# Block sums of two MLP phases on VectorE, RWKV output weights loaded during the scan, two affine maps on ScalarE

## The chip, the core and the metric

The kernel runs on one core of a Trainium2 chip. Its engines work through one instruction queue each, in order: TensorE (PE, with its weight loads listed apart as PEld), VectorE (DVE), ScalarE (ACT), GpSimd (POOL) and SyncE (SP, which issues most DMAs). The metric is the device time of the core in microseconds, as the median of several runs; less is better. The profile is one execution of its own.

## What is computed

The program is a decoder trunk of two layers for 1024 positions of width 1024, all in float32. Layer 0 mixes tokens with an RG-LRU, layer 1 with RWKV-7; each layer then attends to a memory of 256 tokens and ends with an MLP of width 4096:

```python
# every layer: x += post_norm(mixer(pre_norm(x)))
#              x += post_norm(mem_xattn(pre_norm(x), norm(mem)))
#              x += post_norm(sqrelu_mlp(pre_norm(x)))
def sqrelu_mlp(h, w_up, w_down):
    return jnp.square(jax.nn.relu(h @ w_up)) @ w_down

def rwkv7_mixer(x, mu, w_rkv, w0, w1, w2, a0, a1, a2, g1, g2, k_k, k_a, ..., w_o):
    ...
    a = jax.nn.sigmoid(a0 + (xa @ a1) @ a2)
    ...
    k = k * (1.0 + (a - 1.0) * k_a)
    ...
    _, ys = lax.scan(step, state0, seq_inputs)      # one state of 64x64 per head
    ...
    return (out * g) @ w_o
```

## The kernel before

**Float32 by halves.** A product of float32 matrices is made of three matmuls of a reduced format. For that an operand of 128x1024 is split (`split`, L230 to L234): ACT casts it into a high half (L232), and DVE subtracts that from the original for the low half (L233); with `eng` given, another engine does the subtraction. `mm3` (L317 to L319) issues the three matmuls. "A split" is below the DVE or POOL part, "a cast" the ACT part.

**The MLP with seven products.** Both halves of the MLP multiply 2x2 blocks with seven block products instead of eight (p1 to p7). Four of the seven take a sum of blocks as an operand: t1 to t4. In the up half (`cphase`) the sums of the activations are made in `combine_in` (L375 to L422): t1 and t2 on DVE, t3 (L416) and t4 (L420) on POOL, two instructions of 128x1024 each, and `parts` splits each operand once its sum is there. The place where this stands between the phases is called the up seam; L482 and L487 are ACT copies of finished up products there.

In the down half (`mlp`, from L925) there are 4 groups of 7 products; each product is 48 matmuls of 512 columns, in four passes p of 12, one for each of four accumulators. The weights' blocks are loaded by SP (`weights`), the activations' blocks come back from memory (`block`). For the sums t1 to t4 of the weights' blocks `sums` issues two POOL instructions of 128x1024 (L1002), in place, one product ahead of their splits; `parts` splits the two A blocks and the two B blocks of the next product, all on DVE but the second B block of a summed operand, which goes to POOL. After each pass the accumulator is copied (ACT, L1059) or added (DVE, L1061) into `acc`: an evacuation. The sums of activations that are spilled for later groups (`out`, L957 to L962) are made on POOL and stored from POOL's DMA queue; the last of them lie at the start of the down phase.

**What sets the order.** A scheduler orders the instructions, each engine's apart. The lines within `with self.line("down")` are kept in the order of the program on each engine; so the evacuations, the splits and the sums of the down phase stand as they are written.

**RWKV.** `decay` makes the tile a, with the map a = 0.5 a + 0.5 (L1268), and `prep_rest` the factor kp = k_a a + (1 - k_a) (L1289), both on DVE for all 8 tiles f. `evac_r` (L1452) takes the r product out of the accumulator. The v phase makes the v product for f = 0 to 7; then a scan of 16 chunks follows. SP loads a chunk pair's tiles ahead of it (L1559 to L1591, and the z tiles of L1563); in the chunk, DVE (L1739, L1747) and PE (L1715, L1720, L1745, L1753) pass a state on. After the scan `tphase` multiplies with the output weights `b_w_o`. Weights come through a plan of tiles: `take` hands out a tile and `fetch` (L266) loads `depth + ahead` tiles further (SP, L252) and splits `depth` of them. During the v phase three tiles of `b_w_o` are loaded and two of them split; the other five are loaded at the scan's end. All these tiles, the raw ones too, come from one pool of "u" buffers of 128x1024.

Of the kernel before, what the change touches and what calls it, by code (L numbers as in the profile page):

```python
# [9 lines left out]
AF = mybir.ActivationFunctionType  # L10
# [39 lines left out]
class Net:  # L50
# [321 lines left out]
    def combine_in(self, xs, hf, g, B):  # L372
# [40 lines left out]
            nc.vector.tensor_sub(t2[i], b22[i], t1[i])  # L413
        parts("t2", t2)
        for i in range(2):
            nc.gpsimd.tensor_tensor(t3[i], t2[i], b11[i], ALU.subtract)  # L416
        parts("t3", t3)
        parts("b22", b22)
        for i in range(2):
            nc.gpsimd.tensor_tensor(t4[i], b21[i], t2[i], ALU.subtract)  # L420
        parts("t4", t4)
        del B["raw"]  # L422

# [512 lines left out]
    def mlp(self, layer, xt, raw, post, late=None):  # L936
# [58 lines left out]

        def sums(m):

            if m < len(seq) and seq[m][3] in DSUMS:
                f = rows[seq[m][0]]
                o, x, y = DSUMS[seq[m][3]]  # L1000
                for i in range(2):
                    nc.gpsimd.tensor_tensor(f[o][i], f[x][i], f[y][i], ALU.subtract)  # L1002

        def parts(m):

            if m >= len(seq):
                return [lambda: None] * 4
            ab = ops[m] = [], []
            name = seq[m][3]
            fs = rows[seq[m][0]][DSUMS[name][0] if name in DSUMS else {"b11": (0, 0), "b21": (1, 0), "b22": (1, 1)}[name]]  # L1010
            a = [lambda t=t: ab[0].append(self.split(t)) for t in blocks.pop(m)]
            return a + [lambda t=t, e=e: ab[1].append(self.split(t, eng=e))
                        for t, e in zip(fs, (None, nc.gpsimd if name in DSUMS else None))]

        def loads():
            block(0)
# [13 lines left out]
        for m, (g, name, qa, qb, bank, begins, ends, to) in enumerate(seq):  # L1030
# [6 lines left out]
            for i in soon(m, 23):  # L1037
                block(i + 1)
            A, B = ops.pop(m)
            work = [parts(i) for i in soon(m, 24)]  # L1040
            line = lambda: self.line("down")
            for p in range(4):
                with line():
                    for w in work:
                        for i in ((0, 1), (2,), (3,), ())[p]:
                            w[i]()
                if begins:
                    ps[bank, p] = self.bank(p + 1)
                o = ps[bank, p]
                for j in range(4):  # L1050
                    at = slice((j % 2) * 512 + p * 128, (j % 2) * 512 + p * 128 + 128)
                    bt = slice((j % 2) * 512, (j % 2) * 512 + 512)
                    self.mm3(o, [t[:, at] for t in A[j // 2]], [t[:, bt] for t in B[j // 2]],
                             begins and j == 0, ends and j == 3, skip_group_check=True)
                with line():
                    for e, s, new in to:
                        to_ = acc[e][:, p, s]
                        if new and g == 0:
                            nc.scalar.copy(to_, o)  # L1059
                        else:  # L1060
                            nc.vector.tensor_add(to_, to_, o)  # L1061
                if g == 3 and name == "p3":
                    post(p, acc[0][:, p, :])
                if g == 3 and name == "p7" and layer == 1 and p == 3:

                    sq = [self.small(1) for _ in range(2)]
                    nc.scalar.activation(self.unit()[:, right], acc[1][:, 3, right], AF.Square, accum_out=sq[0])
                if g == 3 and name == "p4":
                    if layer == 1 and p == 3:
                        nc.scalar.activation(self.unit()[:, left], acc[1][:, 3, left], AF.Square, accum_out=sq[1])  # L1070
                        nc.gpsimd.tensor_tensor(sq[0], sq[0], sq[1], ALU.add)
                        post(7, acc[1][:, 3, :], sq[0])
                    else:
                        post(4 + p, acc[1][:, p, :])
            with line():
                for i in soon(m, 23):
                    sums(i + 1)
            if m == 1:
                rest()
            if late and m >= LATE:  # L1080
# [120 lines left out]
def rwkv(self, X, xt, lw_wa, lw_g, post):  # L1201
# [55 lines left out]
    def decay(f):  # L1257
# [7 lines left out]
                self.mm3(p, (wa2[0][r, cs], wa2[1][r, cs]), (hwa[0][r, s], hwa[1][r, s]), True, True)  # L1265
                nc.scalar.activation(t[:, s], p, AF.Tanh, bias=c1(b), scale=0.5)
        nc.vector.tensor_scalar(lw, lw, -LC, -LC, ALU.mult, ALU.add)
        nc.vector.tensor_scalar(a, a, 0.5, 0.5, ALU.mult, ALU.add)  # L1268
        IP = self.unit()
        nc.vector.tensor_tensor_scan(IP, d01, lw, 0.0, ALU.mult, ALU.add)  # L1270
        P = lw
# [14 lines left out]
    def prep_rest(f):  # L1286
        a, P, IP, at = dk.pop(f)
        kp = self.unit()
        nc.vector.tensor_scalar(kp, a, self.col("k_a", f), self.kam[:, f:f + 1], ALU.mult, ALU.add)  # L1289
        sq = self.unit()  # L1290
        nc.scalar.activation(sq, at, AF.Square)
        nc.vector.scalar_tensor_tensor(a, a, self.col("k_k", f), IP, ALU.mult, ALU.mult)
# [385 lines left out]
    for i, fs in enumerate(turns):  # L1678
        for f in turns[i + 1] if i < 6 else []:
            early(f)  # L1680
        self.fphase(I["b_w_rkv"][0, 2], fs, xv, evac_v, spread=i == 0)
        aside(len(TURNS) + 6 + i)
        if fs[-1] == LD:
# [5 lines left out]
        scan_scale(c)  # L1689
        scan_gram(c, range(4))  # L1690
    load_late(0)
    self.depth, self.ahead = 2, 3
    self.psum_layout("banks")
    for h in range(2):
        nc.gpsimd.memset(cst[0]["sv"][hr[h], :, h, :], 0.0)
    for c in range(16):
        if c % 2 == 0:
            with (ExitStack() if c else self.behind()):
                load(c // 2 + 1)
                load_solved(c // 2 + 1)  # L1700
                load_late(c // 2 + 1)
        s = cst[c]
        sv, gts, mv, pcc, xtc, pcs = s["sv"], s["gts"], s["mv"], s["pcc"], s["xt"], s["pcs"]
        dbv = self.db[:, 0:128].rearrange("p (q a t) -> p q a t", a=2, t=8)[:, :, c % 2, c // 2:c // 2 + 1]
# [52 lines left out]
        post_mean(c)  # L1757
    post_var(15)
    post_norm(15)
    self.psum_layout("mixed")  # L1760

    self.later += [lambda: flip_out(14), lambda: flip_out(15)]
    w = I["b_w_o"][0]
    rows = []
# [53 lines left out]
```

## Time and profile before

| | |
|---|---|
| time, median of 3 runs | 2984.14 us (2982.08 to 2985.70) |
| the profiled execution | 2987.84 us, span 2986.1 us |
| TensorE's mean granted clock | 0.983 of 2.4 GHz |
| busy, share of the span | PE 96%, PEld 80%, DVE 62%, ACT 45%, POOL 39% |
| down phase of layer 0 | about 1010 to 1360 us |
| up seams | about 710 to 735 and 2355 to 2385 us |
| v phase, scan | about 1640 to 1800, 1800 to 2000 us |
| down phase of layer 1 | about 2660 to 2986 us |

The profile counts microseconds from the start of the span. "Busy" is the time in which an engine executed; a row of the order of time merges like instructions in sequence, and a wait stands in brackets with the instruction that ended it. PEclk is the clock granted to TensorE, 1.00 being 2.4 GHz and 0.50 being 1.2 GHz; a stretch in which both occur has a mean between them. Since PE is busy in all but 4% of the span, the waits of PE are what is to be looked at, each with what ended it.

### The profile page before, as it was taken

To read this page: it belongs to the slowest core of one execution; us is meant where nothing else is said; L and a number is where in the kernel's file an instruction comes from. 1 tells how busy PE (TensorE), PEld (TensorE's weight loads), DVE (VectorE), ACT (ScalarE), POOL (GpSimd) and SP (SyncE) were. 2 spreads that over 40 slices of the span, in tenths; PEclk is the share of its full clock that TensorE was granted. 3 is DMA by queue.
4 is the path that set the end of the run, shared out by engine and by line. 5 is a ranking of instruction groups with operands and counts; after the bars stand their busy time and mean duration, and the time that the engine had idled before them with its cause. 6 is when DMAs were issued, how large, how long until landed. Compare 5 with 4: busy or idle time off the path is not lost. (4 is left out here: it accounts for less than half of the span.)

```text
span 2986.1 us, 42754 instructions
## 1 busy us (share of the span) xinstructions
PE 2860.0 (96%) x16987; PEld 2381.4 (80%) x16987; DVE 1842.6 (62%) x2020; ACT 1349.5 (45%) x1967; POOL 1151.9 (39%) x1055
## 2 busy tenths in 40 slices
PE   7999999999999999999999998999999999999998
PEld 6888798887888878787778677878788788887886
DVE  5576552556455578887685627883355745557878
ACT  6464342545444543347452534442244544454333
POOL 2000110024766554351486215652002466655445
PEclk9999999999999999999999999999999999999999
DMA  7212362123444554432656989852312244455443
GB/s 256 75 50 83 101 196 71 60 74 104 161 150 143 192 196 148 159 116 92 175 162 187 235 228 227 182 136 92 99 52 83 89 155 150 152 203 183 155 169 113
DMA packets 383847, 421.91 MB, mean 141 GB/s; under 512 B 91440, under 2 KB 294432, under 8 KB 383648
## 3 DMA queue, kind: packets, MB, share of 16 engines
q1 hardware_dynamic: 371616, 379.19, 42.3%
q0 software_dynamic: 11568, 39.41, 3.6%
q8 instruction: 133, 2.18, 0.3%
q14 instruction: 66, 0.54, 0.1%
q10 hardware_dynamic: 464, 0.59, 0.1%
HBM read 283.79 MB, written 134.74 MB: 140 GB/s over the span
## 5 line engine op out<-in xcount | busy, mean ns | idle before, releaser
L233 DVE TENSOR_TENSOR u<-u,u 128x1024 fp32r<-128x1024 f32 (+1 forms) x518 | 845.9, 1657 | 360.6 <-ACT u L232 342.3
L232 ACT CAST u<-u 128x1024 fp32r<-128x1024 f32 (+1 forms) x550 | 542.7, 1022 | 405.7 <-POOL u L1002 107.8
L318 PE MATMUL q<-u,u 128*128 128x512 f32 (+2 forms) x1824 | 700.4, 385 | 17.3 <-DVE u L233 17.2
L317 PE MATMUL q<-u,u 128*128 128x512 f32 (+2 forms) x1824 | 694.5, 387 | 13.6 <-ACT u L232 7.5
L319 PE MATMUL q<-u,u 128*128 128x512 f32 (+2 forms) x1824 | 693.6, 384 | 0.5 <-DVE u L233 0.5
L317 PE MATMUL p<-u,u 128*128 128x512 f32 (+1 forms) x1728 | 659.4, 384 | 21.3 <-ACT u L232 9.8
L318 PE MATMUL p<-u,u 128*128 128x512 f32 (+1 forms) x1728 | 657.6, 381 | 6.4 <-DVE u L233 6.4
L319 PE MATMUL p<-u,u 128*128 128x512 f32 (+1 forms) x1728 | 656.0, 380 | 3.7 <-DVE u L233 3.7
L318 PEld LDWEIGHTS q<-u,u 128*128 128x128 f32 (+1 forms) x1824 | 345.9, 190 | 88.6 <-DVE u L233 23.0
L317 PEld LDWEIGHTS q<-u,u 128*128 128x128 f32 (+1 forms) x1824 | 344.7, 189 | 85.9 <-ACT u L232 9.2
L328 POOL TENSOR_SCALAR s<-s 128x1 f32<-128x1 f32 x98 | 40.3, 411 | 941.3 <-ACT u L326 921.8
L317 PEld LDWEIGHTS p<-u,u 128*128 128x128 f32 x1728 | 331.3, 192 | 86.3 <-ACT u L232 13.8
L319 PEld LDWEIGHTS q<-u,u 128*128 128x128 f32 (+1 forms) x1824 | 345.3, 189 | 67.6 <-DVE u L233 0.7
L318 PEld LDWEIGHTS p<-u,u 128*128 128x128 f32 x1728 | 332.1, 192 | 67.9 <-DVE u L233 10.5
L319 PEld LDWEIGHTS p<-u,u 128*128 128x128 f32 x1728 | 331.5, 192 | 65.6 <-DVE u L233 5.2
L1002 POOL TENSOR_TENSOR u<-u,u 128x1024 f32<-128x1024 f32 x64 | 185.3, 2912 | 191.3 <-DVE u L233 165.4
L1061 DVE TENSOR_TENSOR z<-z,q 128x512 f32<-128x512 f32 x192 | 128.1, 679 | 92.3 <-PE q L319 92.3
L430 POOL TENSOR_TENSOR u<-u,u 128x512 f32<-128x512 f32 x96 | 150.9, 1575 | 8.3 <-PE q L318 5.1
L233 POOL TENSOR_TENSOR u<-u,u 128x1024 fp32r<-128x1024 f32 x32 | 80.7, 2523 | 95.3 <-ACT u L232 73.8
L957 POOL TENSOR_TENSOR u<-u,u 128x512 f32<-128x512 f32 x32 | 44.1, 1377 | 154.7 <-ACT u L946 140.5
L319 PE MATMUL q<-z,u 128*128 128x512 f32 x256 | 99.8, 390 | 1.2 <-DVE u L233 1.2
L318 PE MATMUL q<-z,u 128*128 128x512 f32 x256 | 99.6, 389 | 0.0
(258 smaller groups left out, 3458.8 us busy)
## 6 DMA issues: line engine op xcount, KB each, us to landing
u<-d SPq DMA_DIRECT2D x198, 512.0 KB, 4.7
d<-u SPq DMA_DIRECT2D x109, 512.0 KB, 3.3
d<-u POOLq DMA_DIRECT2D x68, 512.0 KB, 3.6
d<-u SPq DMA_DIRECT2D x132, 256.0 KB, 3.4
u<-in_m_w_up SPq DMA_DIRECT2D x64, 512.0 KB, 5.3
u<-in_m_w_down SPq DMA_DIRECT2D x64, 512.0 KB, 7.8
u<-in_c_w_kv SPq DMA_DIRECT2D x32, 512.0 KB, 6.8
u<-d SPq DMA_DIRECT2D x56, 256.0 KB, 6.8
```

The lines of the kernel that those rows point to most:

```text
L232: self.nc.scalar.copy(hv, src)
L233: (eng or self.nc.vector).tensor_tensor(lv, src, hv, ALU.subtract)
L317: mm(o, ah, bh, start=first, stop=False, **kw)
L318: mm(o, ah, bl, start=False, stop=False, **kw)
L319: mm(o, al, bh, start=False, stop=last, **kw)
L328: nc.gpsimd.tensor_scalar(v, ss, 1.0 / n, eps, ALU.mult, ALU.add)
L430: sub = lambda o, x, y: nc.gpsimd.tensor_tensor(o, x, y, ALU.subtract)
L957: tt(s1, r21, r22, ALU.add)
L1002: nc.gpsimd.tensor_tensor(f[o][i], f[x][i], f[y][i], ALU.subtract)
L1061: nc.vector.tensor_add(to_, to_, o)
```

## The change

- In `combine_in`, t3 and t4 are made on DVE.
- In the down phase the sums t1 to t4 are made on DVE, 32 instructions a layer, and the second B blocks are split on DVE as well, 16 a layer. `parts` and `sums` now give lists of work, which is handed out over the four passes: three pieces ahead of pass 0, one ahead of each later pass, what is left after the last. Each piece stands alone in the kept order, so sums and splits stand between the evacuations.
- `decay` makes the map of a on ACT for f above 1, and `prep_rest` makes kp on ACT: 6 and 8 instructions.
- From the v phase's f of 5 on, `depth` and `ahead` are set so that no output weight is fetched there. In the scan, at chunks 5, 7, 9, 11, 13 and 15, they are raised step by step, so that one tile of 128x1024 is loaded at each of the first, and one split at each of the last two; after the scan they have their old values.

```diff
@@ combine_in
-            nc.gpsimd.tensor_tensor(t3[i], t2[i], b11[i], ALU.subtract)
+            nc.vector.tensor_sub(t3[i], t2[i], b11[i])
...
-            nc.gpsimd.tensor_tensor(t4[i], b21[i], t2[i], ALU.subtract)
+            nc.vector.tensor_sub(t4[i], b21[i], t2[i])
@@ mlp: sums, parts
-                for i in range(2):
-                    nc.gpsimd.tensor_tensor(f[o][i], f[x][i], f[y][i], ALU.subtract)
+            return [lambda i=i: nc.vector.tensor_sub(f[o][i], f[x][i], f[y][i]) for i in range(2)]
...
-            a = [lambda t=t: ab[0].append(self.split(t)) for t in blocks.pop(m)]
-            return a + [lambda t=t, e=e: ab[1].append(self.split(t, eng=e))
-                        for t, e in zip(fs, (None, nc.gpsimd if name in DSUMS else None))]
+            return [lambda o=o, t=t: o.append(self.split(t)) for o, ts in zip(ab, (blocks.pop(m), fs)) for t in ts]
@@ mlp: the products
-            work = [parts(i) for i in soon(m, 24)]
+            work = [w for i in soon(m, 24) for w in parts(i)] + [w for i in soon(m, 23) for w in sums(i + 1)]
             line = lambda: self.line("down")
             for p in range(4):
-                with line():
-                    for w in work:
-                        for i in ((0, 1), (2,), (3,), ())[p]:
-                            w[i]()
+                for _ in range(3 if p == 0 else 1):
+                    if work:
+                        with line():
+                            work.pop(0)()
...
-            with line():
-                for i in soon(m, 23):
-                    sums(i + 1)
+            while work:
+                with line():
+                    work.pop(0)()
@@ decay, prep_rest
-        nc.vector.tensor_scalar(a, a, 0.5, 0.5, ALU.mult, ALU.add)
+        if f > 1:
+            nc.scalar.activation(a, a, AF.Copy, scale=0.5, bias=0.5)
+        else:
+            nc.vector.tensor_scalar(a, a, 0.5, 0.5, ALU.mult, ALU.add)
...
-        nc.vector.tensor_scalar(kp, a, self.col("k_a", f), self.kam[:, f:f + 1], ALU.mult, ALU.add)
+        nc.scalar.activation(kp, a, AF.Identity, scale=self.col("k_a", f), bias=self.kam[:, f:f + 1])
@@ v phase
+        if fs[-1] >= 5:
+            self.depth, self.ahead = min(2, 7 - fs[-1]), 0
         self.fphase(I["b_w_rkv"][0, 2], fs, xv, evac_v, spread=i == 0)
...
-    self.depth, self.ahead = 2, 3
@@ scan, in the loop over chunks c
+        if c > 4 and c % 2:
+            n = (c - 3) // 2
+            self.depth, self.ahead = max(0, n - 4), min(n, 4)
+            self.fetch(self.taken - 1)
@@ after the scan
+    self.depth, self.ahead = 2, 3
```

How the order moves, at three places. Names ending in a number are tiles ("u" the common pool, "z" the accumulators `acc`, "q" PSUM, "d" memory); what a row waits for is in brackets, by the counter that it reads: another engine, DMAHW for DMAs of SP, DMASW for DMAs of POOL.

DVE before, in the first group of the down phase of layer 0; u_7864 and u_7865 are the A blocks of the sixth product (p7), u_7387 is the first half of its operand t3:

```order
L233 TENSOR_TENSOR u_7890<-u_7391,u_7889 128x1024 [waits DMASW5_49,DMAHW1_49,DVE_49,Activation_49]
L233 TENSOR_TENSOR u_7907<-u_7392,u_7906 128x1024 [waits DMAHW2_49,DVE_49,Activation_49]
L233 TENSOR_TENSOR u_7943<-u_7864,u_7942 128x1024 [waits DMAHW7_49,PE_49,Activation_49]
L233 TENSOR_TENSOR u_7947<-u_7865,u_7946 128x1024 [waits DMAHW0_49,Activation_49,Pool_49]
L1061 TENSOR_TENSOR z_7614<-z_7614,q_7800 128x512 [waits PE_49]
L233 TENSOR_TENSOR u_7964<-u_7387,u_7963 128x1024 [waits Activation_49]
L1061 TENSOR_TENSOR z_7614<-z_7614,q_7818 128x512 [waits PE_49]
L1061 TENSOR_TENSOR z_7614<-z_7614,q_7836 128x512 [waits PE_49]
```

DVE after, at the same place, from the A blocks of the product ahead on:

```order
L233 TENSOR_TENSOR u_7869<-u_7788,u_7868 128x1024 [waits DMAHW5_49,Activation_49]
L233 TENSOR_TENSOR u_7873<-u_7789,u_7872 128x1024 [waits DMASW4_49,DMAHW6_49,Activation_49,Pool_49]
L233 TENSOR_TENSOR u_7877<-u_7391,u_7876 128x1024 [waits DMASW5_49,Activation_49]
L233 TENSOR_TENSOR u_7894<-u_7392,u_7893 128x1024 [waits DVE_49,Activation_49]
L1002 TENSOR_TENSOR u_7387<-u_7391,u_7387 128x1024 [waits DMASW3_49,DMASW0_49]
L1002 TENSOR_TENSOR u_7388<-u_7392,u_7388 128x1024
L233 TENSOR_TENSOR u_7943<-u_7864,u_7942 128x1024 [waits DMAHW7_49,DMASW6_49,Activation_49]
L233 TENSOR_TENSOR u_7947<-u_7865,u_7946 128x1024 [waits DMAHW0_49,PE_49,Activation_49]
L233 TENSOR_TENSOR u_7951<-u_7387,u_7950 128x1024 [waits PE_49,Activation_49]
L1060 TENSOR_TENSOR z_7614<-z_7614,q_7804 128x512 [waits PE_49]
L233 TENSOR_TENSOR u_7968<-u_7388,u_7967 128x1024 [waits DMASW7_49,Activation_49,Pool_49]
L1060 TENSOR_TENSOR z_7614<-z_7614,q_7822 128x512 [waits PE_49]
```

The two sums of t3 now stand on DVE ahead of the A splits, the split out of u_7387 stands ahead of the first evacuation and not behind it, and the split out of u_7388, on POOL before, stands behind that evacuation.

POOL before, at the same place (the spill sums L957 to L961 and their stores L959 and L962 are those of the last chunks of the up phase):

```order
L960 TENSOR_TENSOR u_7781<-u_7401 128x512
L1002 TENSOR_TENSOR u_7379<-u_7391,u_7379 128x1024
L1002 TENSOR_TENSOR u_7380<-u_7392,u_7380 128x1024
L958 TENSOR_TENSOR u_7772<-u_7772,u_7330 128x512
L958 TENSOR_TENSOR u_7780<-u_7780,u_7401 128x512
L233 TENSOR_TENSOR u_7833<-u_7380,u_7832 128x1024
L1002 TENSOR_TENSOR u_7387<-u_7391,u_7387 128x1024
L1002 TENSOR_TENSOR u_7388<-u_7392,u_7388 128x1024
L959 DMA d_5373<-u_7772 128x2x512
L961 TENSOR_TENSOR u_7773<-u_7331,u_7772 128x512
L959 DMA d_5373<-u_7780 128x2x512
```

POOL after, at the same place:

```order
L960 TENSOR_TENSOR u_7781<-u_7401 128x512
L958 TENSOR_TENSOR u_7772<-u_7772,u_7330 128x512
L958 TENSOR_TENSOR u_7780<-u_7780,u_7401 128x512
L959 DMA d_5373<-u_7772 128x2x512
L961 TENSOR_TENSOR u_7773<-u_7331,u_7772 128x512
L959 DMA d_5373<-u_7780 128x2x512
```

The four sums and the split that stood between the spill sums and their stores are gone; the stores follow the spill sums at once.

SP before, in the scan, at a chunk pair's loads:

```order
L1591 DMA u_15359<-d_10060 128x8x128
L1591 DMA u_15360<-d_10061 128x8x128
L1563 DMA z_14285<-d_10063 64x8x128 x4
L1559 DMA u_15718<-d_10064 128x8x64 x2
L1559 DMA u_15721<-d_10064 128x8x64 x2
```

SP after, at the same place:

```order
L1593 DMA u_15345<-d_10060 128x8x128
L1593 DMA u_15346<-d_10061 128x8x128
L1565 DMA z_14268<-d_10063 64x8x128
L252 DMA u_15527<-in_b_w_o 64x1024 x2
L1565 DMA z_14268<-d_10063 64x8x128 x3
L1561 DMA u_15707<-d_10064 128x8x64 x2
L1561 DMA u_15710<-d_10064 128x8x64 x2
```

An output-weight tile, in two halves, now stands among the z loads of the chunk pair and ahead of its other loads; this is so at four chunk pairs, and a fifth tile stands behind the last pair's loads.

## Rows read from the trace of the kernel before

**Rows 1.** The page: engine totals, and the group of evacuations.

```profile
PE 2860.0 (96%) x16987; PEld 2381.4 (80%) x16987; DVE 1842.6 (62%) x2020; ACT 1349.5 (45%) x1967; POOL 1151.9 (39%) x1055
...
L1061 DVE TENSOR_TENSOR z<-z,q 128x512 f32<-128x512 f32 x192 | 128.1, 679 | 92.3 <-PE q L319 92.3
```

**Rows 2.** Waits of PE over the span: sum in us, how many, the longest.

```profile
PE q L318 <- DVE u L233: 17.2, 8, 5.4
```

**Rows 3.** PE in order of time, start and us, at the two longest waits.

```profile
1071.34 0.79 PE L318 MATMUL q<-u,u 128*128 128x512 f32 x1 [5.35 <-DVE u L233]
...
2720.60 0.80 PE L318 MATMUL q<-u,u 128*128 128x512 f32 x1 [5.35 <-DVE u L233]
```

**Rows 4.** Stretches: length, busy us (xstarts) by engine, then PEclk, DMA share, GB/s.

```profile
1060.00:1080.00 20.00, 14.65 (x53) 11.53 (x52) 16.94 (x10) 4.69 (x5) 8.98 (x4) 0.83 0.83 332
1080.00:1330.00 250.00, 245.16 (x1078) 201.53 (x1077) 203.52 (x187) 97.94 (x108) 112.87 (x64) 0.99 0.40 135
1519.00:1571.00 52.00, 46.61 (x294) 37.41 (x293) 50.97 (x47) 28.79 (x41) 45.64 (x45) 0.97 0.53 159
1650.00:1800.00 150.00, 138.39 (x1188) 105.85 (x1181) 63.60 (x93) 65.19 (x102) 34.41 (x48) 0.97 0.92 237
1220.50:1223.70 3.20, 3.14 (x8) 2.49 (x8) 3.20 (x5) 0.78 (x1) 0.00 (x0) 0.50 0.85 261
```

**Rows 5.** DVE, then POOL, in order of time ahead of the first long wait.

```profile
1044.91 6.48 DVE L233 TENSOR_TENSOR u<-u,u 128x1024 fp32r<-128x1024 f32 x2 [2.69 <-ACT u L232]
...
1056.91 10.82 DVE L233 TENSOR_TENSOR u<-u,u 128x1024 fp32r<-128x1024 f32 x2
...
1058.08 1.45 POOL L962 DMA_DIRECT2D d<-u  x2
1059.55 2.42 POOL L233 TENSOR_TENSOR u<-u,u 128x1024 fp32r<-128x1024 f32 x1
1061.90 4.74 POOL L1002 TENSOR_TENSOR u<-u,u 128x1024 f32<-128x1024 f32 x2
```

**Rows 6.** Lines L233, L1002 and L962: ns min/median/max; landing of L962's stores.

```profile
L233 DVE TENSOR_TENSOR u<-u,u x518: 677/1221/8595, 16.8 to 2952.0; 128x1024 fp32r<-128x1024 f32 x164, 128x512 fp32r<-128x512 f32 x9
...
L1002 POOL TENSOR_TENSOR u<-u,u x64: 2386/3320/3410, 1009.6 to 2934.4; 128x1024 f32<-128x1024 f32 x64
...
DMA to landing us min/median/max: 3.1/3.2/9.5
```

**Rows 7.** The stretch 1080 to 1330 again: L233 alone (DVE, POOL), L1002 alone.

```profile
1080.00:1330.00 250.00, 133.37 (x78) 30.57 (x12) 0.99 0.40 135
...
1080.00:1330.00 250.00, 68.56 (x24) 0.99 0.40 135
```

**Rows 8.** Waits of PE from 1080 to 1330.

```profile
PE q L318 <- DVE u L233: 4.8, 3, 2.0
```

**Rows 9.** Up seams in order of time: ACT, DVE and PE of layer 0, PE of layer 1.

```profile
722.36 2.00 ACT L232 CAST u<-u 128x1024 fp32r<-128x1024 f32 x2 [5.61 <-POOL u L416]
...
713.40 18.95 DVE L233 TENSOR_TENSOR u<-u,u 128x1024 fp32r<-128x1024 f32 x8
...
724.89 0.50 PE L317 MATMUL q<-u,u 128*128 128x512 f32 x1 [1.72 <-ACT u L482]
...
2372.63 0.50 PE L317 MATMUL q<-u,u 128*128 128x512 f32 x1 [2.19 <-ACT u L482]
```

**Rows 10.** DVE and PE in order of time, ahead of the r product.

```profile
1551.58 1.18 DVE L1289 TENSOR_SCALAR u<-u,colt,kam 128x1024 f32<-128x1024 f32 x1
...
1560.49 0.47 PE L317 MATMUL p<-u,u 128*128 128x512 f32 x1 [1.96 <-DVE u L1452]
```

**Rows 11.** Scan: PE, SP in order of time; waits of SP from 1860 to 1980.

```profile
1820.86 1.86 PE L1616 MATMUL q<-z,u 128*128 128x128 f32 x8 [5.00 <-DMA u<-d]
...
1973.83 8.70 SPq L252 DMA_DIRECT2D u<-in_b_w_o  x10
...
SPq L1563 <- PE q L1616: 27.5, 8, 7.7
SPq L252 <- POOL u L1671: 18.0, 1, 18.0
```

More of the change, by code (lines that the diff above doesn't have):

```diff
@@ L996, in sums @@
         def sums(m):
-            if m < len(seq) and seq[m][3] in DSUMS:
-                f = rows[seq[m][0]]
-                o, x, y = DSUMS[seq[m][3]]
-                for i in range(2):
-                    nc.gpsimd.tensor_tensor(f[o][i], f[x][i], f[y][i], ALU.subtract)
+            if m >= len(seq) or seq[m][3] not in DSUMS:
+                return []
+            f = rows[seq[m][0]]
+            o, x, y = DSUMS[seq[m][3]]
+            return [lambda i=i: nc.vector.tensor_sub(f[o][i], f[x][i], f[y][i]) for i in range(2)]
         def parts(m):
             if m >= len(seq):
-                return [lambda: None] * 4
+                return []
             ab = ops[m] = [], []
```

## The prediction

> **What bounds the kernel now.** I read the engine totals first [rows 1]: TensorE (PE) is busy for 2860.0 of 2986.1 us, VectorE (DVE) for 62%, GpSimd (POOL) for 39%. So PE sets the end, and an edit is worth what PE waits, plus what PE then loses at the half clock. The table of PE's waits [rows 2] says who ends them: splits on DVE (L233) head it, 17.2 us in 8 waits, the longest 5.4. Then I went place by place.
>
> The two longest, one in each down phase, are alike: PE waits 5.35 us for a DVE split [rows 3], and behind it the granted clock falls. At 0.50, that is at 1.2 instead of 2.4 GHz, 8 matmuls start in 3.2 us, 0.40 us apart; at a clock of 0.99, 1078 take 245.16 us, 0.227 apart [rows 4]. In the 20 us from 1060, clock 0.83, only 53 start [rows 4] where 20 / 0.227 = 88 would: 35 x 0.227 = 8.0 us are lost, two thirds of it the wait, the rest the clock.
>
> Why the split was late: DVE's two splits from 1056.91 took 10.82 us and ended at 1067.73 [rows 5]. POOL was at a split and two block sums from 1059.55 to 1066.64 then (the last two are the row of 4.74 us, [rows 5]). The whole population says the same: DVE's split has a median of 1.221 and a maximum of 8.595 us; POOL's block sum (L1002) takes 2.386 at least and 3.320 at the median [rows 6]. An operation of either engine is stretched when the other one runs. The longest is not only that: it ended 1.1 us, its own length, after POOL's second sum, and its row in the order (out of u_7865) has POOL's count among its waits (shown with the change).
>
> The Trainium skill ("SBUF — State Buffer", section "SBUF: two separate sides") calls the stretching an exclusive lock on a shared port pair: the operation that starts first keeps it until it ends, be it a DVE operation with two SBUF inputs or a GpSimd one. By that rule a split can lose one POOL operation, 1.22 + 2.39 = 3.6 us; the 8.595 is more, so by the rule, too, the rest is a wait for POOL's queue. The third rival follows from it.
>
> **The change, part by part.**
>
> *Down phases.* 64 sums and 32 splits go from POOL to DVE. What that does to DVE's load is read from one stretch, 1080 to 1330: DVE's 78 splits take 133.37 us there, 1.71 each; POOL has 24 sums and 12 splits [rows 7]. After the change DVE has 78 + 12 + 24 = 114 operations of that size; at 1.22 they take 139.1 us. DVE's load rises by 5.7 us, from 203.5 to 209 of 250 [rows 4], 84%: the work is all but paid for by the collisions that it ends. If none of them went, it would be 203.5 + 36 x 1.22 = 247 of 250, and DVE would be the bound. I take the first, since POOL keeps only the spill sums (L957 to L961), which end with the phase's first products.
>
> At the two stalls: in the order of the changed kernel nine operations of DVE stand from the split out of u_7788 to the late one, out of u_7387 (shown with the change). DVE began the first of them at 1044.91 [rows 5]. Nine at 1.22 end at 1055.9. If four of them still meet a spill sum and take 3.24 (6.48 for two, [rows 5]), they end at 1064.0. PE wants the result at 1066 (1071.34 less the wait, [rows 3]). Both ends are in time, so the wait goes and its clock loss with it: 2 x 8.0 = 16. Bounds: -16, and 0 if the wait comes back in another place. I take **-15**.
>
> Inside the phase of layer 0 PE has three smaller waits for such splits, 4.8 us in all, the longest 2.0 [rows 8], and behind that one 3.2 us at half clock [rows 4], 1.4 lost. Together 6.2; layer 1 has little of that kind. Against it stand DVE's 84%, and one late product that now carries 8 splits, 2 sums and 4 evacuations: 10 x 1.22 + 4 x 0.68 [rows 1] = 14.9 us of DVE beside 48 matmuls, 48 x 0.227 = 10.9 us. PE wants none of that product's results at once, but some of it may come back. Bounds -6.2 and +3; **-5**.
>
> *Up seams.* Four sums a layer go to DVE. Now the ACT cast of t3 waits 5.61 us for POOL's L416, a copy (L482) stands behind it, and PE waits 1.72 for that copy; in layer 1 it waits 2.19 [rows 9]. A wait of that length drew a half-clock piece in the down phase (1.4). DVE's eight splits take 18.95 us [rows 9]. After: 8 splits and 4 sums, 12 x 1.22 = 14.6, so the last operand comes earlier. The second split of t2 has four sums ahead of it, and two splits at 2.37 become two splits and four sums, 7.3: up to 2.6 us later than now, unless the first splits too were collided ones. What PE does then hides some of it. In all 1.72 + 2.19 = 3.9, and 1.4 for the clock; bounds -5.3 and +1; **-4**, the waits that the rows show.
>
> *Affine maps to ScalarE.* 14 maps leave DVE, at most 1.18 us each [rows 10]. ACT takes them; it is busy for 28.8 of 52 us where DVE is for 51.0 [rows 4]. One lies ahead of a wait: the 1.18 us at 1551.58, in a row of DVE work without a pause up to L1452, for which PE waits 1.96 [rows 10]. That falls to 0.8, perhaps with a half-clock piece behind it (1.4). On ACT, a map of about 1.0 us (its casts, 2.00 for two, [rows 9]) can stand ahead of a cast that PE wants. Bounds -2.6 and +2; **-1.5**.
>
> *Output weights.* Three loads of 512 KB and two splits leave the v phase, where the queues carry 237 GB/s at a busy share of 0.92 [rows 4]: 1.5 MB are 6.6 us of that traffic. But the wait there that a load ended, 5.00 us up to 1820.86 [rows 11], was for a chunk load that SP issued long behind those weights. In the scan five loads come, one in two chunks, ahead of the chunk loads; SP needs 0.9 us for one (8.70 for ten halves, [rows 11]). At the scan's end two or three splits still stand among the last chain of DVE. Bounds -6.6 (all of that traffic) and +5.7 (five loads of 0.9 and one split of 1.2 on the path); **-1.5**.
>
> **Sum.** -15 - 5 - 4 - 1.5 - 1.5 = -27 us. The profiled execution took 2987.84, 3.7 above the median of 2984.14 (0.12%), so I apply the sum to the median: **2957**; from the profiled one it would be 2961.
>
> **The rivals.**
>
> *DVE becomes the bound of the down phases.* For it: 247 of 250 us if the collisions persist, and sums, splits and evacuations now share one queue in order, so that an evacuation behind a split that waits for its cast holds its accumulator. Against it: the 84%, and a POOL with nearly nothing left there. Price: the -5 is lost, and the late product costs 14.9 - 10.9 = 4 in each layer: -15 - 4 - 3 + 8 = -14, **2970**.
>
> *The start stalls only move.* The late split's other half, on POOL until now, (out of u_7388) stands behind an evacuation after the change. If PE waits half as long there, it is -8 instead of -15: **2964**.
>
> *The start stalls stay, through POOL's stores.* After the change the sum into u_7387 and the splits out of u_7864 and u_7388 wait for POOL's stores (DMASW). Now POOL issues its last two from 1058.08, [rows 5]; such a store takes 3.2 us to land at the median and 9.5 at most [rows 6], so they are there between 1061.3 and 1068.3. If they came no earlier, the five operations from that sum to the late split would end between 1067.4 and 1074.4, and now the split ends at 1071.3. The -15 is lost: **2972**. This is where the reading by the skill's rule leads, a stall that hangs on POOL's queue. Against it: four block sums and a split stand among the spill sums in POOL's order before and none after (shown with the change), 4 x 3.3 + 2.4 = 16 us, so the stores come some 16 us earlier.
>
> *Slower: the scan's chunk loads come late.* SP works in order. Before, an output-weight load waits 18.0 us for its buffer, once, with nothing urgent behind it [rows 11]. Now such a load stands ahead of chunk loads five times. SP idles up to 7.7 us in a wait for z there [rows 11]; a buffer that comes free later than that delays the chunk, and PE waits as at 1820.86, 5.00 us, and loses 1.4 at the clock: 5 x 6.4 = +32, in sum +5 to +6: **2990**. It decides from a wait of about 7 us at that load. Against it: nothing is held through the scan now that was not held before (there, three of the weights were).
>
> *Nothing that shows.* DVE is the bound and the start stalls stay: -14 + 15, **2985**.
>
> **Chances.** Forecast (2950 to 2962) 0.50; the stalls move (2962 to 2967) 0.13; DVE the bound (2967 to 2975) 0.13; the stalls stay (2969 to 2976) 0.08; nothing that shows 0.05; slower 0.06; every term near its lower bound (-16 - 6.2 - 5.3 - 2.6 - 6.6 = -37, 2947) 0.05. The range 2947 to 2973 leaves out about 2 in 10. A measurement of this kernel tells some 0.2%, 6 us, from nothing: faster 0.50 + 0.13 + 0.13 + 0.08 + 0.05 = 0.89, the same 0.05, slower 0.06.
>
> **What would show it.** Right: no wait of PE over 1 us in the first products of the down phases, and a granted clock of 1.00 over those 20 us; the DVE split's maximum under 4 us; eight splits and four sums in about 15 us at the up seam; PE's waits for L233 down by some 15 us. Wrong: PE waits for an evacuation (L1061's successor) or a cast in groups 1 to 3 of a down phase; PE waits for a chunk load in chunks 5 to 13 while SP is held at a weight load; DVE without a pause through a down phase.

## The result

The changed kernel takes 2955.32 us at the median of 4 runs (2951.64 to 2958.01), the kernel before 2983.11 (2980.26 to 2985.70): a ratio of 0.9906, with a 95% interval of 0.9889 to 0.9923, or 28 us less. 2957 was forecast. Two of the runs told of below were far longer at a much lower granted clock (4051.84 us at 0.653, 3185.37 at 0.846) and are left out of the medians.

The profiled execution of the changed kernel has a span of 2956.3 us, 29.8 less than before. Its page and PE's waits answer to [rows 1] and [rows 2]; first the engine totals, then the wait that headed PE's list before (sum, how many, the longest):

```profile
PE 2846.8 (96%) x16987; PEld 2373.4 (80%) x16987; DVE 1807.8 (61%) x2110; ACT 1365.6 (46%) x1981; POOL 860.7 (29%) x951
...
PE q L318 <- DVE u L233: 0.4, 1, 0.4
```

POOL lost 291 us of busy time. DVE got 104 operations from it, gave up 14 maps, and is busy 35 us *less*. PE's waits at L318 for a DVE split fell from 17.2 us to 0.4.

Both traces have the same 16,987 instructions on PE, so the place of a gain can be read by comparing the start of the k-th one in each. This table is worked out that way from the two traces (the place by the clock of before):

| stretch of before, us | what lies there | difference, us | forecast |
|---|---|---|---|
| 720 to 740 | up seam of layer 0 | -2.3 | |
| 2365 to 2380 | up seam of layer 1 | -4.1 | -4 both |
| 1060 to 1080, 2700 to 2730 | the two long waits | -8.3, -8.0 | -15 |
| 1200 to 1310, 2940 | smaller waits of the down phases | -7.6, -1.3 | |
| 1310 to 1375 | last products of layer 0, first of layer 1 | +3.9 | -5 with the row above |
| 1375 to 1650 | RWKV's first products | -4.5 | -1.5 |
| 1650 to 2010 | v phase, scan, start of the output product | +1.9 | -1.5 |

The stretches of the changed kernel that answer to [rows 4]: 20 us at the place of each long wait, then the same 1078 matmuls as before; and DVE's splits and sums (L233, L1002) in the last one, alone. Columns as in [rows 4].

```profile
1050.00:1070.00 20.00, 20.00 (x90) 16.58 (x89) 15.12 (x16) 11.24 (x12) 0.00 (x0) 1.00 0.61 225
2690.00:2710.00 20.00, 20.00 (x90) 16.56 (x89) 15.41 (x17) 6.57 (x8) 0.00 (x0) 1.00 0.32 109
...
1069.50:1312.50 243.00, 243.00 (x1078) 201.27 (x1077) 198.44 (x222) 96.60 (x107) 10.71 (x14) 1.00 0.40 137
...
1069.50:1312.50 243.00, 104.69 (x89) 1.00 0.40 137
...
1069.50:1312.50 243.00, 29.14 (x24) 1.00 0.40 137
```

90 matmuls now start in 20 us where 53 did [rows 4], and the granted clock is 1.00. In the long stretch 113 splits and sums take 104.69 + 29.14 = 133.8 us of DVE, where 78 splits took 133.4 before [rows 7].

### The profile page after: what moved, and what is told of

Its sections match the earlier page's. It is cut to its first block, busy times and chain, and to the rows that moved or that the text cites. A ratio compares the mean times of both kernels' runs of the same rounds, so it can differ in the third digit from the quotient of the medians.

```text
span 2956.3 us, 42688 instructions
## 1 busy us (share of the span) xinstructions
PE 2846.8 (96%) x16987; PEld 2373.4 (80%) x16987; DVE 1807.8 (61%) x2110; ACT 1365.6 (46%) x1981; POOL 860.7 (29%) x951
## 4 chain that ended last, share of the span: by engine, by line
PE 83%; DVE 7%; DMA 3%; issue 2%; ACT 2%; POOL 2%; SPq 1%; DVEq 0%; POOLq 0%; ACTq 0%
PE q L317 15%; PE q L319 15%; PE q L318 15%; PE p L317 11%; PE p L319 11%; PE p L318 11%; DVE u L233 2%; DMA u<-d 1%; PE q L1618 1%; DVE u L1158 1%; POOL u L1732 1%; ACT u L232 1%; PE q L358 0%; PE q L908 0%; PE q L383 0%
## 5 line engine op out<-in xcount | busy, mean ns | idle before, releaser
L233 DVE TENSOR_TENSOR u<-u,u 128x1024 fp32r<-128x1024 f32 (+1 forms) x550 | 741.5, 1379 | 354.0 <-ACT u L232 331.9
L318 PE MATMUL q<-u,u 128*128 128x512 f32 (+2 forms) x1824 | 697.9, 383 | 1.1 <-POOL u L365 0.5
L318 PE MATMUL p<-u,u 128*128 128x512 f32 (+1 forms) x1728 | 655.5, 379 | 5.9 <-DVE u L233 5.8
L318 PEld LDWEIGHTS q<-u,u 128*128 128x128 f32 (+1 forms) x1824 | 344.0, 189 | 68.7 <-DVE u L233 2.8
L318 PEld LDWEIGHTS p<-u,u 128*128 128x128 f32 x1728 | 330.8, 191 | 67.5 <-DVE u L233 9.6
L319 PE MATMUL q<-z,u 128*128 128x512 f32 x256 | 99.8, 390 | 1.2 <-DVE u L233 1.2
L318 PE MATMUL q<-z,u 128*128 128x512 f32 x256 | 99.6, 389 | 0.0
L317 PE MATMUL q<-z,u 128*128 128x512 f32 x256 | 99.3, 389 | 0.0
L639 DVE SCALAR_TENSOR_TENSOR u<-p,s,u 128x1024 f32<-128x1024 f32 x24 | 30.8, 1284 | 109.1 <-ACT u L232 69.6
L957 POOL TENSOR_TENSOR u<-u,u 128x512 f32<-128x512 f32 x32 | 44.2, 1382 | 175.7 <-ACT u L946 158.5
```

What stands on the lines that cost most here:

```text
L233: (eng or self.nc.vector).tensor_tensor(lv, src, hv, ALU.subtract)
L317: mm(o, ah, bh, start=first, stop=False, **kw)
L318: mm(o, ah, bl, start=False, stop=False, **kw)
L319: mm(o, al, bh, start=False, stop=last, **kw)
L639: nc.vector.scalar_tensor_tensor(o, src, r, gb, ALU.mult, ALU.mult)
L957: tt(s1, r21, r22, ALU.add)
```

## The experiments

### Each edit alone

**Down phases.** All of `mlp`'s edit, nothing else of the diff.

> The kernel before with the down phases' edit alone (sums and second B splits on DVE, handed out over the passes). Theory (POOL's operations stretch DVE's, and DVE has room without them): both start waits of 5.35 us and their clock loss go, 16.3 us, and the smaller waits inside, 8.8 us; about 4 us come back behind the last products of layer 0, where DVE's order changes. In all -21 us, that is 2962. Rival (the edits help each other: the down phase is early because the up seam feeds it sooner): less than 15 us, over 2968.

Measured: 2962.53 us against 2983.75, ratio 0.9923 (0.9905 to 0.9942), 21 us less. By place: -8.3 and -8.0 at the long waits, -7.6 and -1.3 at the smaller ones, and +2.6 from 1310 to 1375. Expected were 2962 and this pattern, with about 4 us coming back in the last stretch. The edit stands by itself.

**Up seams.**

> The kernel before with t3 and t4 of the up seams on DVE, nothing else. Theory: the two waits of PE for the copy behind the cast of t3 go, 1.72 and 2.19 us, and the half clock behind the second: -2.3 us in layer 0 and -4.1 in layer 1, read place by place, -6.4 in all. Rival (part of that came from the down phase's edit): the first seam gives 2.3, the second under 2.5.

One run: 2978.76. By place -2.3 at the first seam, -4.2 at the second, and 1.4 in all from 740 to 1375. The waits for the copy are gone. But the second seam also lost 1.4 to 2.2 us in five kernels which don't touch it (maps alone, weights alone, and three of the variants below), and 0.0 with the down edit alone: that is the half-clock piece behind the seam, which the profile of before happened to have. The waits themselves are worth the 3.9 us that they take in [rows 9].

**Affine maps.**

> The kernel before with the two affine maps on ACT alone. Between 1375 and 1650 us the changed kernel gains 4.5 us. Theory (the maps do it, by shortening DVE's row ahead of the r product and ahead of the gram's split): -4.5 us in that stretch here too. Rival (an earlier start shifted what the clock sees, and DMA with it): -1.5 us or less here, the rest belongs to no edit.

One run: 2984.01. From 1375 to 1650 it gains 1.2 us, not 4.5. The rival holds. What the maps do can be seen at PE's wait for L1452 [rows 10]: it is 1.2 to 1.3 us in all seven traces of this study with the maps on ACT, and 1.9 to 2.0 in the seven without. Over the stretch the seven gain between 1.0 and 5.0 us, the six others of a changed kernel lie between -0.9 and +0.2. Half-clock pieces come and go there (the trace of before has four, that of the changed kernel one), 1.4 us each; three pieces fewer make 4.2 of the 4.5 us, and no run shows that they belong to the edit.

**Output weights.**

> The kernel before with the output weights' loads moved into the scan alone. Theory (the chunk loads set the time at the v phase's end, and the scan's end is no shorter): from 1650 to 2010 us it loses 1 to 2 us as the changed kernel does (+1.9 there), 2984 to 2985. Rival (the traffic saved in the v phase helps, and the loss in the changed kernel comes from arriving earlier at a fixed load): -1 to -6 us in that stretch, 2977 to 2982.

Measured: 2984.72 against 2983.75, ratio 1.0004 (0.9994 to 1.0013): nothing that can be told. The other way round:

> The changed kernel without the move of the output weights. Theory (the move costs 1 to 2 us): 1 to 2 us under the changed kernel, 2953 to 2954, with the gain in the stretch from the v phase to the scan's end. Rival (the move is worth its place, and the loss seen there belongs to the earlier arrival): 1 to 4 us above it, 2956 to 2959.

Measured: 2956.48, ratio to before 0.9913 (0.9891 to 0.9935), that of the changed kernel being 0.9906. The number lies in the rival's range, but only 1 us from the changed kernel's, so it speaks for neither. By place, from 1650 to 2010, it is +0.5 with the move alone, +0.4 without it and +1.9 in the changed kernel; two more kernels below that have the move give +1.3 and -3.5. So the move makes no difference that these runs resolve, and the +1.9 is not shown to be its price. The trace shows why little could be had. PE's wait for the chunk load and SP's issues there, and the scan's waits of SP, to be held against [rows 11]:

```profile
1803.29 2.08 PE L1618 MATMUL q<-z,u 128*128 128x128 f32 x8 [5.74 <-DMA u<-d]
...
SPq L1565 <- PE q L1618: 23.5, 8, 6.1
SPq L252 <- PE q L1745: 11.0, 1, 11.0
```

The wait that a chunk load ends is 5.74 us now and was 5.00: PE comes to it 18.3 us earlier than before, and the load lands 17.6 us earlier. One weight load still waits long for its buffer, 11.0 us, but no chunk of PE's waits behind it: the chunk pairs' period is 24.2 us in both traces. At the scan's end three splits still stand in DVE's last chain:

```profile
1972.47 0.86 DVE L1755 TENSOR_TENSOR u<-u,q 64x256 f32<-64x256 f32 x2
1973.37 1.23 DVE L233 TENSOR_TENSOR u<-u,u 128x1024 fp32r<-128x1024 f32 x1
1974.62 0.87 DVE L1755 TENSOR_TENSOR u<-u,q 64x256 f32<-64x256 f32 x2
...
1976.85 1.21 DVE L233 TENSOR_TENSOR u<-u,u 128x1024 fp32r<-128x1024 f32 x1
1977.98 0.87 DVE L1747 TENSOR_TENSOR u<-q,db 64x256 f32<-64x256 f32 x2
...
1979.66 1.21 DVE L233 TENSOR_TENSOR u<-u,u 128x1024 fp32r<-128x1024 f32 x1
1980.90 0.88 DVE L1747 TENSOR_TENSOR u<-q,db 64x256 f32<-64x256 f32 x2
```

### What held the late split up

Three kernels take the down phase's start apart. First the sums alone on DVE, the second B splits back on POOL:

```diff
+ pool = lambda o, n: nc.gpsimd if o is ab[1] and n and name in DSUMS else None
- return [lambda o=o, t=t: o.append(self.split(t)) for o, ts in ... for t in ts]
+ return [lambda o=o, t=t, n=n: o.append(self.split(t, eng=pool(o, n))) for o, ts in ... for n, t in enumerate(ts)]
```

> The down phases' edit alone, but only the sums on DVE: the second B block of a summed operand is still split on POOL. Theory (any POOL operation stretches DVE's split by one operation of its own length): POOL keeps 32 operations of 2.4 us, DVE's longest split in the down phase is 3.6 us, the start waits are under 1 us, and of the 25 us that the edit takes away 18 to 23 stay. Rival (a row of POOL operations is needed to hold DVE up): nothing is lost, 24 to 25.

One run: 2957.17. By place: -8.3 and -8.0 at the long waits, -7.6 and -1.3 at the smaller, -0.9 from 1310 to 1375. PE's waits for L233 at that matmul are 0.5 us. So the sums alone give all of it, and without the price behind the last products. My theory expected 18 to 23; the rival was nearer. POOL has nothing to do here from 1048.29 to 1057.00, behind its last stores.

Then the second B splits alone on DVE, the sums back on POOL (`nc.gpsimd.tensor_tensor` in the list of `sums`):

> The down phases' edit alone, but only the second B splits on DVE: the sums stay on POOL, two back to back. Theory (a POOL operation stretches DVE's by one operation, whatever follows it): longest DVE split in the down phase 3.6 us, start waits 1 us or less, mid-phase waits about as before. Rival (POOL's operations in a row hold DVE up until the row ends): a DVE split of 5 to 6 us beside the two sums (2 x 2.4 + 1.2), start waits of 2 to 4 us.

One run: 2970.97. The long waits go here as well, -8.3 and -7.7 by place, but not the smaller ones: the stretch from 1080 to 1310 gives -0.2 in place of -7.6.

```profile
PE q L318 <- DVE u L233: 7.4, 8, 3.0
```

This is what the theory said: DVE's longest split in the down phases takes 3.43 us, no start wait is left, and from 1080 to 1310 PE waits 4.8 us for splits as before [rows 8]. But it is no test of the rival's row behind the stores, since handing out the pieces changed POOL's order too. Its sums stand ahead of the last stores now, and behind these it does nothing up to 1080:

```profile
1047.51 1.53 POOL L961 TENSOR_TENSOR u<-u,u 128x512 f32<-128x512 f32 x1
1049.00 3.37 POOL L1002 TENSOR_TENSOR u<-u,u 128x1024 f32<-128x1024 f32 x1
1052.31 0.72 POOL L959 DMA_DIRECT2D d<-u  x1
...
1054.55 1.45 POOL L962 DMA_DIRECT2D d<-u  x2
```

So both kernels, by different ways, leave no row of POOL operations behind the last stores, and the long wait goes in full; the smaller waits go only with the sums. What stands ahead of that row? The stores of the spill sums, which POOL issues itself [rows 5]. The third kernel leaves POOL's sums and splits as they were and issues only the stores L959 and L962 from ACT's queue:

```diff
- nc.gpsimd.dma_start(to[:, 3:5], half(st[0]))
+ nc.scalar.dma_start(to[:, 3:5], half(st[0]))
- nc.gpsimd.dma_start(to[:, 5:7], half(st[1]))
+ nc.scalar.dma_start(to[:, 5:7], half(st[1]))
```

> The kernel before with the stores of the spill sums issued from ACT's DMA queue and not from POOL's; the sums stay on POOL. The longest DVE splits of the kernel before (8.6 us twice in the down phases, 4.6 to 5.3 us 18 times in the up phases) all stand beside rows of POOL operations that follow a store issued by POOL. Theory (the store at POOL's queue is part of it: without it DVE and POOL take turns): the longest split is 3.5 us, and the start waits of 5.35 us fall to about 1. Rival (the row of POOL operations is enough): splits of 5 us and 8 us stay, and so do the start waits.

One run: 2964.34, 20 us under the 2984.04 of before on the same chip, with no arithmetic moved. The long waits are gone (-8.3 and -8.0 by place), the smaller ones are mostly there (-1.5 in place of -7.6). The splits of this kernel, to be held against [rows 6], and DVE and POOL in order of time at the place of the first long wait:

```profile
L233 DVE TENSOR_TENSOR u<-u,u x518: 676/1220/3439, 16.8 to 2928.5; 128x1024 fp32r<-128x1024 f32 x164, 128x512 fp32r<-128x512 f32 x9
...
1056.94 2.36 DVE L233 TENSOR_TENSOR u<-u,u 128x1024 fp32r<-128x1024 f32 x2 [0.69 <-ACT u L232]
...
1062.89 4.84 DVE L233 TENSOR_TENSOR u<-u,u 128x1024 fp32r<-128x1024 f32 x2
1067.65 0.68 DVE L1061 TENSOR_TENSOR z<-z,q 128x512 f32<-128x512 f32 x1
1068.25 2.82 DVE L233 TENSOR_TENSOR u<-u,u 128x1024 fp32r<-128x1024 f32 x1
...
1059.89 3.43 POOL L233 TENSOR_TENSOR u<-u,u 128x1024 fp32r<-128x1024 f32 x1 [5.63 <-issue]
1063.27 6.72 POOL L1002 TENSOR_TENSOR u<-u,u 128x1024 f32<-128x1024 f32 x2
```

The maximum is 3.439 us where it was 8.595. The split that took 8.6 us, out of u_7865, is the second of the row at 1056.94. It is done before POOL's split begins at 1059.89, so at this place it met no row at all; why POOL begins later is not shown. What does collide there goes by turns: the two POOL sums at 1063.27 take 6.72 us, 3.36 each, so POOL is stretched too. Before, the same two took 4.74, 2.37 each [rows 5], their shortest time, and DVE got nothing. That the stores are what makes a collision long is to be read where the same operations of POOL meet a split with its stores and without them, in the up phases. There the kernel before has 20 long splits (the expectation counted 18; one of them takes 6.33 us), and this one has none. The same edit on the changed kernel:

> The changed kernel with the spill sums' stores issued from ACT's DMA queue, nothing else. Theory (a store issued by POOL is what lets a row of POOL operations hold DVE off): the 20 splits of 4.6 to 5.3 us, all in the up phases, fall to 3.5 or less; the time is that of the changed kernel within 2 us, since PE does not wait for them. Rival (rows of POOL operations are enough): the 20 long splits stay.

One run: 2953.04. The changed kernel, whose POOL does no sums in the down phases, still had 20 long splits, all in the up phases; with the stores on ACT there is none. First the changed kernel (all splits; then one long split with POOL beside it), then the splits of this one:

```profile
L233 DVE TENSOR_TENSOR u<-u,u x550: 677/1219/5317, 16.8 to 2923.8; 128x1024 fp32r<-128x1024 f32 x176, 128x512 fp32r<-128x512 f32 x8
...
850.81 5.04 DVE L233 TENSOR_TENSOR u<-u,u 128x1024 fp32r<-128x1024 f32 x1 [7.11 <-ACT u L232]
...
849.54 0.73 POOL L959 DMA_DIRECT2D d<-u  x1 [0.41 <-POOL u L958]
850.28 1.31 POOL L961 TENSOR_TENSOR u<-u,u 128x512 f32<-128x512 f32 x1
851.53 1.30 POOL L431 TENSOR_TENSOR u<-u 128x512 f32<-128x512 f32 x1
852.79 1.29 POOL L430 TENSOR_TENSOR u<-u,u 128x512 f32<-128x512 f32 x1
854.01 0.74 POOL L962 DMA_DIRECT2D d<-u  x1
```

```profile
L233 DVE TENSOR_TENSOR u<-u,u x550: 677/1220/2365, 16.8 to 2918.9; 128x1024 fp32r<-128x1024 f32 x176, 128x512 fp32r<-128x512 f32 x8
```

The picture at 850 is the one at 1059 in small: POOL issues a store, then three operations at their full speed, and DVE's split, which starts in the first, ends only 1.1 us, its own length, after the store that follows the third. The theory held in both kernels as to the splits; the time is 2.3 us under the changed kernel's, of which 1.7 have a place (below).

The traces make the theory narrower than I wrote it. In each of the eleven with POOL's stores, 20 splits of the up phases begin beside the first operation behind a store, and all 20 are held: they end behind POOL's whole row. A split that begins beside the second operation gets the next turn: 1.29 us at 759.73 in the kernel before. So does one that begins beside the first of several operations with no store ahead of it. The kernel before has 13 such behind an idle POOL, with 3.07 us at most (first row below, then POOL beside it). And in the kernel with the splits alone on DVE a split got its turn right behind a store (second view): it began beside the L961 at 1047.51 (above), which a split of DVE's had itself held up (1.53 us for 1.30), and the sum behind that was stretched to 3.37.

```profile
1207.35 3.07 DVE L233 TENSOR_TENSOR u<-u,u 128x1024 fp32r<-128x1024 f32 x1
...
1206.94 2.40 POOL L233 TENSOR_TENSOR u<-u,u 128x1024 fp32r<-128x1024 f32 x1 [4.12 <-ACT u L232]
1209.30 3.37 POOL L1002 TENSOR_TENSOR u<-u,u 128x1024 f32<-128x1024 f32 x1
```

```profile
1047.81 2.31 DVE L233 TENSOR_TENSOR u<-u,u 128x1024 fp32r<-128x1024 f32 x1
```

So a store of POOL's own makes the collision long for a split that begins beside the operation right behind it, if that operation was not held up itself, or, as at 1059, beside the store; without such a store the longest split is that of one turn.

### The price behind the last products, and what was worth its place

> The changed kernel with the second B splits of the last group of the down phases back on POOL, the others on DVE. Theory (those splits disturb the order of DVE at the end of the phase: evacuations and row statistics): from 1310 to 1375 us the loss of 3.9 us of the changed kernel goes, 2951 to 2953 in all. Rival (the handing out of the pieces does it, wherever the splits are): the loss stays at 3 us or more there.

The edit is that of the sums-only kernel, with `and seq[m][0] == 3` in its condition, on the changed kernel. One run: 2950.64. From 1310 to 1375 it gains 1.1 us, where the changed kernel loses 3.9. The second B splits of the last group were the price. DVE in order of time, in the changed kernel and then in this one, from the same row statistics on (L639, L640 and L647 make a row of the result; the next layer's transposes wait for the last L647):

```profile
1306.86 1.28 DVE L639 SCALAR_TENSOR_TENSOR u<-z,s,u 128x1024 f32<-128x1024 f32 x1
1308.86 0.76 DVE L647 TENSOR_SCALAR u<-u,s 128x1024 f32<-128x1024 f32 x1 [0.72 <-POOL s L330]
1309.53 0.68 DVE L1060 TENSOR_TENSOR z<-z,q 128x512 f32<-128x512 f32 x1
1310.12 1.22 DVE L640 TENSOR_TENSOR u<-u,u 128x1024 f32<-128x1024 f32 x1
```

```profile
1305.31 1.29 DVE L639 SCALAR_TENSOR_TENSOR u<-z,s,u 128x1024 f32<-128x1024 f32 x1 [0.44 <-POOL s L330]
1306.52 0.68 DVE L1062 TENSOR_TENSOR z<-z,q 128x512 f32<-128x512 f32 x1
1307.11 1.22 DVE L640 TENSOR_TENSOR u<-u,u 128x1024 f32<-128x1024 f32 x1
1308.25 0.75 DVE L647 TENSOR_SCALAR u<-u,s 128x1024 f32<-128x1024 f32 x1
```

In the changed kernel L640 stands behind an L647 that waits 0.72 us for POOL's statistics, and comes 3.3 us after its L639; here it is 1.8. Behind the first of these orders PE waits 1.05 and 0.52 us, and the rest is lost at the seam and to the clock behind it.

Last, what was worth its place in one kernel: the sums of the down phases, the seams' sums and the maps moved, the second B splits and the output weights left; and the same with the stores on ACT.

> The kernel before with the sums of the down phases, the up seams' sums and the affine maps moved as in the changed kernel; the second B splits stay on POOL and the output weights where they were. Theory (the splits need no move, and moving them costs the 2.6 to 3.9 us behind the last products of layer 0; the weights give nothing): 3 to 5 us under the changed kernel, 2950 to 2953. Rival (POOL's splits collide in the middle of the down phase and cost what the tail gives): 2954 to 2957.

> The same with the spill sums' stores issued from ACT's DMA queue. Theory (the stores matter only where PE waits for a split behind them, and no such place is left): within 1 us of it, while the 4.6 to 5.3 us splits of the up phases go. Rival (those long splits of the up phase delay PE through the weights' sums): 2 us or more faster. Other rival (issuing on ACT holds casts up): 1 us or more slower.

Measured on the same chip, against 2982.94 of before: 2952.09, ratio 0.9888 (0.9869 to 0.9907), and 2950.08, ratio 0.9890 (0.9870 to 0.9909). Both are 3 to 5 us under the changed kernel's 2955.32; the intervals overlap its 0.9889 to 0.9923, so the order of the three is likely, not shown. These times cannot tell the two apart either, but the traces can: the long splits in the up phases (20 in the first, none in the second) do cost PE something, at two places. In the kernel before the first long split of each up phase ends at 783.98 and 2433.22, and PE waits for it there:

```profile
784.03 0.50 PE L319 MATMUL q<-z,u 128*128 128x512 f32 x1 [0.52 <-DVE u L233]
...
2433.27 0.50 PE L319 MATMUL q<-z,u 128*128 128x512 f32 x1 [0.63 <-DVE u L233]
```

All three kernels with the stores on ACT gain 0.8 and 0.9 us at these two matmuls, and the ten others that were changed gain nothing there. So the first rival is right that the long splits delay PE, if only at two of the 20 and not by way of the weights' sums: 1.7 us in all.

## Why the prediction was right

The sum was -27 and the medians differ by 28. The largest term was right, and so was the way of the gain: POOL's operations taken away, DVE's splits are no longer stretched, and PE no longer waits for them. That the total came out so near is in part luck, since the errors of the other terms cancel.

- **The long waits, -15: measured -16.3.** The picture was right: no wait over 1 us is left there, the clock is 1.00, and DVE's split was done at 1057.1 (below), 6.7 us before PE's place for it (1066 less 2.2).

```profile
1042.69 4.63 DVE L233 TENSOR_TENSOR u<-u,u 128x1024 fp32r<-128x1024 f32 x4 [3.59 <-ACT u L232]
1047.24 2.35 DVE L1002 TENSOR_TENSOR u<-u,u 128x1024 f32<-128x1024 f32 x2
1053.57 3.50 DVE L233 TENSOR_TENSOR u<-u,u 128x1024 fp32r<-128x1024 f32 x3 [3.98 <-ACT u L232]
```

These are the nine operations that I summed back to back. None of them meets POOL, but DVE waits 3.98 us for a cast among them, which the sum left out.

The cause behind it was half right. I read the 8.6 us split as a wait for POOL's queue, since its row lists POOL's count and one POOL operation could not explain it. With the stores on ACT the same split, with the same count to wait for, is done before POOL's row begins (the row at 1056.94 above), so that count does not hang on the row. It was stretched by three POOL operations, which the rule of the Trainium skill ("SBUF — State Buffer", section "SBUF: two separate sides"), as I applied it, does not give; with the stores off POOL the rows fit it (3.439 us at most, one turn).
- **DVE's load, +5.7: measured -5.1** (203.5 to 198.4 us over the same 1078 matmuls). 113 operations at 1.18 us, since pipelined ones follow each other at 1.14, are half of the difference; the other half lies in DVE's other operations there and was not looked into. That DVE has room when the collisions go was the step that decided the sign of the whole, and it held. The rival of DVE as the bound fell with it; so did that of POOL's stores, which the changed kernel issues some 30 us earlier (before at 1058.08 [rows 5]):

```profile
1026.50 1.45 POOL L962 DMA_DIRECT2D d<-u  x2
```

- **Smaller waits, -5: -8.9, and +3.9 at the tail.** Both lie outside the bounds (-6.2 and +3); that together they make -5.0 is luck. The price of one crowded late product was foreseen, "up to 3"; what it was made of was not: not DVE's load, but the place of one operation in DVE's order.
- **Up seams, -4: -6.4**, beyond the bound of -5.3. Of it the waits are 3.9, as forecast; the rest goes with half-clock pieces that come and go. Eight splits and four sums took 13.7 us (713.42 to 727.13) where "about 15" was said.

```profile
713.42 1.22 DVE L416 TENSOR_TENSOR u<-u,u 128x1024 f32<-128x1024 f32 x1
...
719.10 8.03 DVE L233 TENSOR_TENSOR u<-u,u 128x1024 fp32r<-128x1024 f32 x7
```

- **Maps, -1.5: -1.2 alone**, of which 0.7 is the wait that was named, 1.96 to 1.2 us (0.8 was said); in the 4.5 of the changed kernel's trace the rest goes with the clock.
- **Output weights, -1.5: +1.9 by the trace, +0.04% (-0.06 to +0.13) alone.** I had counted traffic as time. PE's wait there hangs on one chunk load, which kept its distance to PE within 0.7 us (a wait of 5.00 us before, 5.74 after); the runs show nothing for this term. The rival of late chunk loads did not come.

## What to carry to other kernels

Ask of every operation on GpSimd what it does to VectorE's beside it, and count the two together: 36 operations came to VectorE in one stretch here, and it was busy for less time than before. Move the least that breaks the row: the sums alone gave all of the gain, and the splits moved with them cost 4 us through the order of the queue they joined. And test a reading of one long row by taking away what stands next to it, not only what is in it: moving only the stores beside the sums cured the long stalls as well. Then look whether the collision was shortened or merely no longer took place.

## What the runs showed of the hardware

A DMA that GpSimd issues changes how GpSimd and VectorE share. Where a VectorE split began beside GpSimd's store or beside the first operation right behind it, GpSimd's next three operations ran at full speed (1.3 us for 128x512, 2.4 us for 128x1024), and the split took 4.6 to 8.6 us instead of 1.22, 22 times in the kernel before. Splits that began beside a later operation, or beside a row with no store ahead, got the next turn. With the stores issued by ScalarE both engines were stretched by turns wherever they met, and no split took over 3.44 us. Why a store does that is not shown. The second thing is the size of what the clock does by itself: half-clock pieces of 1.4 us came and went between traces at places that no edit touched, so a difference below some 2 us at one place of one trace is no evidence; one that all traces with an edit show and none without it (the 0.8 us above) is.
